# Up projection of an encoder layer: a third seven-product pair in every second group, and both transposed sets of a group in one place

## The chip, the cores and the metric

The kernel runs on one core of a Trainium2 chip. The metric is the device time of one execution in microseconds, taken as the median of several runs. The engines are TensorE (PE in the profile, with its weight loads shown as PEld), VectorE (DVE), ScalarE (ACT), GpSimd (POOL) and SyncE (SP), which here only issues DMAs.

## The reference

One layer of an encoder on 256 tokens of width 2048, all in float32. The part that matters here is the last one, the squared-ReLU MLP between two RMS norms; ahead of it come two attention branches with gates.

```
h = rms_norm(x, norm_mix_pre)
proj = h @ w_in                       # q, k, v of two attentions, two gates
oa, on = diff_attention(...), neighbourhood_attention(...)
mixed = sigmoid(g_a) * (oa @ w_branch_a) + sigmoid(g_b) * (on @ w_branch_b)
x = x + rms_norm(mixed @ w_out, norm_mix_post)
h = rms_norm(x, norm_mlp_pre)
u = square(relu(h @ w_up))            # w_up is 2048 x 8192
x = x + rms_norm(u @ w_down, norm_mlp_post)
```

## The kernel before, in words

**Products.** Each float32 operand is split into a high part that TensorE takes in its rounded format and a low part, the rest. A product of two operands is then three matmuls: high by high, high by low, low by high (`Products.add`, L695 to L706). A matmul here has 128 x 128 elements of the activations as its stationary operand and 128 x 512 of the weights as its moving one.

**Groups and pairs.** The up projection (L1100 to L1149) runs over eight groups of 1024 columns of `w_up`. In a group it runs over eight *pairs*: a pair is 256 of the 2048 rows, a weight tile of 128 x 4 x 512 (1 MB), and both token halves. A pair is taken in one of two ways. As a light pair (`eight`, L720) it has eight products, so 24 matmuls, into four PSUM banks. As a heavy pair (`seven`, L708) it is a 2 x 2 block product by the scheme of Strassen and Winograd: seven products, 21 matmuls, into seven banks, of which four (0, 4, 5, 6) belong to heavy pairs alone. For it VectorE has to form sums of the weight blocks (`pair_weights`, L644 to L660), and sums of the activations have to be there (`sums_of`, L768, kept in `h2sum`).

**The weights of a pair.** `pair_weights` (L633) loads the raw tile by a DMA on SyncE's queue. For a light pair ScalarE makes the high part (L640) and VectorE the low part (L642). For a heavy pair three quarters of the tile are split so (L645, L649), and four sums of 512 columns are made by VectorE (L646 to L648, tile `t`) and split as well (L658 by ScalarE into `eh`, L659 by VectorE into `el`). There are three buffers each for the raw, the high and the low tile. The split sums lie in the pool `mid` of five buffers, four to a heavy pair, unless a `low` is given: then the two low sums lie there. `Weights.next` (L672) asks for the weights of two pairs ahead of the one to be computed.

**The end of a group.** After the last heavy pair of a group `combine` (L726) puts the heavy banks together into the tile `z` with one copy by ScalarE and four adds by VectorE (L729 to L733). After the last light pair `u_piece` (L1094) adds each of the four light banks to `z` on VectorE (L1097) and applies ReLU and the row's scale on ScalarE (L1098). The next group's light products need these four banks.

**Transposes.** The down projection needs the squared result with its columns on the partitions. While group g runs, `u_sets` (L1076) does this for the two 512-column halves of group g - 1: eight TensorE transposes into two PSUM banks for each half (L1084), a square by ScalarE (L1087), then the splits and, for the even half, the sums of the down projection's heavy pairs (`act_sets`, L1019), and DMAs on GpSimd's queue that keep the results in device memory (L1046). The banks of the transposes come from the pool of four that also holds the heavy pairs' own banks.

**Pages.** Most working tiles, `z`, the transposed sets, the weight sums `t` and the `h2sum` among them, come from one pool of 27 buffers of 4 KB a partition (`page`).

**Order.** The list `UPS` (L1100) gives the pairs of a group in order, each with 1 if it is heavy; group 0 takes all its pairs light (`ALL8`). In `wide_group` (L735) a place n of that list first calls for weights, then `each(n)` (here `up_each`, L1123, which calls `u_sets` in the second and third place), then the products. Each engine's queue is ordered when the program is built, by the kernel's order and a simulated timeline; at run time each queue goes in its order, and waits by semaphores. So matmuls of neighbouring pairs can stand mixed in TensorE's queue.

Of the kernel before, what the change touches and what calls it, by code (L numbers as in the profile page):

```python
# [50 lines left out]
def encoder_layer(ctx: ExitStack, tc: tile.TileContext, a, out):  # L51
# [13 lines left out]
    def page(shape, dt, name):  # L65
        return pages.tile(shape, dt, tag="pg", name=name)
# [7 lines left out]
    def bank(name, big=False):  # L74
        if big:
            return mm.tile([P, 512], F32, tag="mm", name=name)
        return ms.tile([P, 512], F32, tag="ms", name=name)
# [602 lines left out]
    def columns(src, i, c):  # L680
        return src[i * T : (i + 1) * T, c : c + 1024].rearrange("(k p) c -> p k c", p=P)
# [53 lines left out]
    def wide_group(name, kinds, weights, stat7, stat8, mm_banks, z, piece, each=None, turn=None, after={}, in_order=False):  # L735

        any7 = any(s for _, s in kinds)
        pr = Products(name, mm_banks)  # L740
        pr.in_order = in_order
        for n, (i, seven) in enumerate(kinds):
            w = weights.next(after)
            if each:
                each(n)
            if seven:
                final = not any(s for _, s in kinds[n + 1 :])
                pr.seven(partial(stat7, i), w, final)
                if final:
                    pr.combine(z)  # L750
                continue
            end = n == len(kinds) - 1
            if turn and n < 2:
                ahead = [*ahead, (i, w)] if n else [(i, w)]
                for t in range(2) if n else ():
                    for ii, ww in ahead:
                        for which in (2 * t, 2 * t + 1):
                            pr.eight(partial(stat8, ii), ww, which, False)
                    if not t:
                        turn()  # L760
                continue
            for which in range(4):
                pr.eight(partial(stat8, i), w, which, end)
                if end:
                    b, t, half = PLAIN[which]
                    piece(t, half, pr.ps[b], any7)

    def sums_of(p1, p2, name):  # L768

        a11, a21, a12, a22 = p1[:, :P], p1[:, P:], p2[:, :P], p2[:, P:]  # L770
        s = page([P, 4, P], F32, f"{name}s")
        nc.vector.tensor_sub(s[:, 0], a21, a22)
        nc.vector.tensor_sub(s[:, 1], a11, a21)
        nc.vector.tensor_sub(s[:, 2], s[:, 0], a11)
        nc.vector.tensor_add(s[:, 3], a12, s[:, 2])
        parts_ = page([P, 2, 4, P], F32R, name)
        nc.scalar.copy(parts_[:, 0], s)
        nc.vector.tensor_sub(parts_[:, 1], s, parts_[:, 0].bitcast(F32))
        return parts_
# [24 lines left out]
    ALL8 = [(i, 0) for i in range(8)]  # L804
# [193 lines left out]
    def first_up(n):  # L998
        for t, c in {2: [(1, 1), (0, 2)], 3: [(1, 2), (0, 3)], 4: [(1, 3)]}.get(n, ()):
            residual_parts(t, c)  # L1000
        if n == 5:
            for t in range(2):
                mlp_squares(t)
                mlp_scale(t)
            for i in range(4):
                kd = dram.tile([P, 1024], F32, name=f"keepx{i}", tag=f"keepx{i}")
                nc.gpsimd.dma_start(kd, x2[i])
                kept["x", i] = kd
# [10 lines left out]
    def act_sets(cg, u):  # L1019


        srcs = []
        if seven_of(cg):
            a11, a21 = u[:, 0:2, :P], u[:, 0:2, P:]
            a12, a22 = u[:, 2:4, :P], u[:, 2:4, P:]
            sums = page([P, 4, 2, P], F32, f"sm{cg}")
            nc.vector.tensor_sub(sums[:, 0], a21, a22)
            nc.vector.tensor_sub(sums[:, 1], a11, a21)
            nc.vector.tensor_sub(sums[:, 2], sums[:, 0], a11)
            nc.vector.tensor_add(sums[:, 3], a12, sums[:, 2])  # L1030
            own = [(slice(0, 1), a11.unsqueeze(1)),
                   (slice(1, 3), u[:, 2:4].rearrange("p k (t q) -> p t k q", t=2))]
            if cg in FIRST:
                own.append((slice(3, 4), a21.unsqueeze(1)))
            srcs = [([P, 1 + len(own), 2, P], own), ([P, 4, 2, P], [(slice(0, 4), sums)])]
        else:
            srcs = [([P, 4, T], [(slice(0, 4), u)])]
        got = []
        for i, (shape, pieces) in enumerate(srcs):
            hi, lo = page(shape, F32R, f"ah{cg}{i}"), page(shape, F32R, f"al{cg}{i}")  # L1040
            for at, src in pieces:
                nc.scalar.copy(hi[:, at], src)
                nc.vector.tensor_sub(lo[:, at], src, hi[:, at].bitcast(F32))
            for n, part in (("h", hi), ("l", lo)):
                kd = dram.tile(shape, F32, name=f"keep{n}{cg}{i}", tag=f"keep{n}{cg}{i}")
                nc.gpsimd.dma_start(kd, part.bitcast(F32))  # L1046
                kept[cg, i, n] = (shape, kd)
            got.append([hi, lo])
        return got
# [26 lines left out]
    def u_sets(cg, z):  # L1076

        u = page([P, 4, T], F32, f"u{cg}")
        for b in range(2):
            pt = bank(f"uT{cg}{b}")  # L1080
            for j in range(2):
                for t in range(2):
                    c = (b * 2 + j) * P
                    nc.tensor.transpose(  # L1084
                        pt[:, j * T + t * P : j * T + (t + 1) * P], z[t][:, cg % 2, c : c + P], ident
                    )
            nc.scalar.activation(  # L1087
                u[:, b * 2 : b * 2 + 2], pt.rearrange("p (j q) -> p j q", j=2), AF.Square
            )
        got = act_sets(cg, u)  # L1090
        if NG - 4 <= cg < NG - 2:
            sets[0, cg] = got
# [4 lines left out]
            nc.vector.tensor_add(zt, zt, ps)  # L1097
        nc.scalar.activation(zt, zt if summed else ps, AF.Relu, scale=r2[:, t : t + 1])  # L1098

    UPS = [(0, 0), (1, 0), (2, 0), (3, 1), (4, 0), (5, 1), (6, 0), (7, 0)]  # L1100
    uw = Weights()
    for g in range(DFF // 1024):
        for i, seven in UPS if g else ALL8:
            uw.ask(columns(a["w_up"], i, g * 1024), f"u{g}_{i}", seven)
    wd = a["w_down"].rearrange("(g h j p) c -> p h g j c", h=2, j=2, p=P)

    blocks = [[NG - 4] + list(range(0, NG - 4, 2)) + [NG - 2], [NG - 2] + list(range(0, NG - 2, 2))]
# [11 lines left out]
    uz = None  # L1119
    for g in range(DFF // 1024):  # L1120
        z = Late(lambda g=g: [page([P, 2, 512], F32, f"u{g}{t}") for t in range(2)])

        def up_each(n, g=g, uz=uz):  # L1123
            if not g:
                first_up(n)
                if n == 7:
                    for i in (3, 5):
                        f = page([P, 2, T], F32, f"h2f{i}")
                        for k in range(2):
                            d = hT2[i][:, k].bitcast(F32)  # L1130
                            nc.vector.tensor_add(f[:, k], d[:, :T], d[:, T:])
                        h2sum[i] = sums_of(f[:, 0], f[:, 1], f"h2s{i}")
            elif n in (1, 2):
                u_sets(g * 2 - 3 + n, uz)

        wide_group(
            f"u{g}",
            UPS if g else ALL8,
            uw,
            h2stat7,  # L1140
            h2stat8,
            (1, 2, 3, 7),
            z,
            partial(u_piece, z=z),
            each=up_each,
            turn=None if g else turn_rows,
            after={} if g else {1: tail[1][1], 2: scaled[0]},
        )
        uz = z  # L1149
# [149 lines left out]
```

## Time and profile before

| | |
|---|---|
| runs | 1358.05, 1360.42, 1361.4 us; median 1360.42 us |
| profiled execution | 1359.99 us, span of its trace 1358.2 us |
| granted TensorE clock | 0.996, mean over the span |
| matmul instructions | 6336 |
| device memory traffic | 335.85 MB, mean 247 GB/s |
| VectorE, ScalarE busy | 1031.9 us, 716.9 us |

The span runs from the first to the last instruction; the profiled execution's own time has 1.8 us around it. In rows of groups the columns are: line, engine, operation, output<-inputs, shapes, count, then busy time and mean of one in ns, then idle time of the engine ahead of them with what ended it. In rows of a timeline they are: start, duration, engine, line and so on, with idle time in brackets. In rows of the chain of waits: start, duration, engine, tile, line, count. L12 is line 12 of the kernel.

### The profile page before, as it was taken

Reading aid. Unit: us, or ns where it says so; the run is one execution under the profiler, and the core shown is the slowest. Engines: PE = TensorE matmul, PEld = TensorE weight load, DVE = VectorE, ACT = ScalarE, POOL = GpSimd, SP = SyncE. Lnnn points to the kernel's source line nnn. Section 1 sums busy time; section 2 is a strip of 40 time slices with the busy share of each in tenths; the row PEclk is TensorE's granted clock in tenths of the full one; section 3 lists DMA queues with packets and bytes.
Section 4 is the critical chain, followed back from the end, with each engine's and each line's share of the span. In section 5 each row is a group of like instructions: output and inputs, shape, how many; then the busy total and the mean of one; then the engine's idle time right before and its main releaser. Section 6 shows DMA issues by size and latency. Waiting matters only on the chain.

```text
span 1358.2 us, 16184 instructions
## 1 busy us (share of the span) xinstructions
PE 1339.8 (99%) x6336; PEld 1120.5 (82%) x6336; DVE 1031.9 (76%) x1176; ACT 716.9 (53%) x841; POOL 38.1 (3%) x71
## 2 busy tenths in 40 slices
PE   8999999999999999999999999999999999999996
PEld 7888888888888888888788888878888888888885
DVE  6878866767867886655777887787888988788886
ACT  6655454545644454344575655556565545555452
POOL 0000000000000000000100000000000000000000
PEclk9999999999999999999999999999999999999999
DMA  9774745574556655575668767776699998799894
GB/s 316 256 235 163 206 159 174 168 205 154 191 186 199 216 204 186 185 281 187 212 204 287 239 227 261 271 248 232 248 322 335 372 358 336 273 361 371 313 370 179
DMA packets 116588, 335.85 MB, mean 247 GB/s; under 512 B 16928, under 2 KB 17440, under 8 KB 116512
## 3 DMA queue, kind: packets, MB, share of 16 engines
q1 hardware_dynamic: 95888, 264.03, 56.8%
q10 hardware_dynamic: 13904, 45.10, 8.7%
q0 software_dynamic: 6720, 25.69, 4.7%
q8 instruction: 49, 0.80, 0.2%
q14 instruction: 27, 0.22, 0.0%
HBM read 307.01 MB, written 29.61 MB: 248 GB/s over the span
## 4 chain that ended last, share of the span: by engine, by line
PE 90%; DMA 5%; DVE 2%; ACT 2%; issue 1%; SPq 0%; ACTq 0%; DVEq 0%; POOLq 0%
PE p L702 24%; PE u L702 21%; PE ga L702 6%; PE gb L702 6%; PE ba L702 3%; PE bb L702 3%; PE qn_p L212 2%; PE kn_p L212 2%; PE y_p L255 2%; PE y_p L254 2%; PE y_p L256 2%; DMA u_0r<-in_w_up 2%; PE qn_p L214 1%; PE kn_p L214 1%; PE ka_p L212 1%; PE qa_p L212 1%
## 5 line engine op out<-in xcount | busy, mean ns | idle before, releaser
L138 DVE TENSOR_TENSOR y_l<-y_w,y_h 128x1024 fp32r<-128x1024 f32 x32 | 37.9, 1222 | 30.9 <-ACT y_h L133 30.9
L133 ACT CAST y_h<-y_w 128x1024 fp32r<-128x1024 f32 x32 | 32.1, 1051 | 40.9 <-PE y_p L256 32.5
L212 PE MATMUL ka_p<-hT,ka_h 128*128 128x512 f32 x128 | 46.9, 410 | 3.3 <-DVE rope_s L281 3.3
L254 PE MATMUL y_p<-y_h,mh 128*128 128x512 f32 x128 | 50.1, 391 | 0.0
L255 PE MATMUL y_p<-y_l,mh 128*128 128x512 f32 x128 | 49.9, 390 | 0.0
L256 PE MATMUL y_p<-y_h,ml 128*128 128x512 f32 x128 | 49.8, 390 | 0.0
L702 PE MATMUL u<-u_0h,h2T 128*128 128x512 f32 x128 | 44.5, 392 | 1.7 <-DVE u L1097 1.6
L212 PE MATMUL qn_p<-hT,qn_h 128*128 128x512 f32 x128 | 45.9, 400 | 0.0
L212 PE MATMUL kn_p<-hT,kn_h 128*128 128x512 f32 x128 | 45.4, 398 | 0.0
L212 PE MATMUL qa_p<-hT,qa_h 128*128 128x512 f32 x128 | 44.9, 407 | 0.4 <-DVE hT L293 0.3
L702 PE MATMUL u<-u_1h,h2T 128*128 128x512 f32 x128 | 44.0, 397 | 0.0
L702 PE MATMUL u<-u_6h,h2T 128*128 128x512 f32 x128 | 41.8, 389 | 0.0
L702 PE MATMUL u<-u_2h,h2T 128*128 128x512 f32 x128 | 41.7, 396 | 0.0
L702 PE MATMUL u<-u_7h,h2T 128*128 128x512 f32 x128 | 41.7, 389 | 0.0
L702 PE MATMUL u<-u_4h,h2T 128*128 128x512 f32 x128 | 41.2, 391 | 0.0
L214 PE MATMUL ka_p<-hT,ka_l 128*128 128x256 f32 x128 | 36.1, 287 | 0.0
L214 PE MATMUL qn_p<-hT,qn_l 128*128 128x256 f32 x128 | 35.9, 281 | 0.0
L214 PE MATMUL kn_p<-hT,kn_l 128*128 128x256 f32 x128 | 35.7, 280 | 0.0
L640 ACT CAST u_1h<-u_1r 128x2048 fp32r<-128x2048 f32 x8 | 15.3, 1916 | 35.6 <-PE u L702 31.6
L214 PE MATMUL qa_p<-hT,qa_l 128*128 128x256 f32 x128 | 33.3, 281 | 0.3 <-DVE qa_l L138 0.3
L212 PEld LDWEIGHTS ka_p<-hT,ka_h 128*128 128x128 f32 x128 | 24.7, 194 | 9.3 <-DVE rope_s L281 3.6
L642 DVE TENSOR_TENSOR u_0l<-u_0r,u_0h 128x2048 fp32r<-128x2048 f32 x8 | 18.3, 2292 | 17.0 <-ACT u_0h L640 17.0
(1379 smaller groups left out, 4364.3 us busy)
## 6 DMA issues: line engine op xcount, KB each, us to landing
y_w<-in_w_out SPq DMA_DIRECT2D x16, 1024.0 KB, 5.2
bh<-keeph ACTq DMA_DIRECT2D x30, 512.0 KB, 9.4
bl<-keepl ACTq DMA_DIRECT2D x30, 512.0 KB, 11.1
keeph<-ah POOLq DMA_DIRECT2D x18, 512.0 KB, 8.0
keepl<-al POOLq DMA_DIRECT2D x18, 512.0 KB, 9.0
ka_w<-in_w_in SPq DMA_DIRECT2D x8, 1024.0 KB, 6.4
va_w<-in_w_in SPq DMA_DIRECT2D x8, 1024.0 KB, 5.2
qn_w<-in_w_in SPq DMA_DIRECT2D x8, 1024.0 KB, 5.2
```

The costliest lines, as they stand in the source:

```text
L133: nc.scalar.copy(hi[part], raw[part])
L138: sub = nc.vector.tensor_sub(lo[part], raw[part], hi[part].bitcast(F32)).ins
L212: nc.tensor.matmul(ps[b], hi[:, k % 4, cs], mv, start=(k == 0), stop=False)
L214: nc.tensor.matmul(ps[b][:, :T], lo[:, k % 4, cs], mv[:, :T], start=False, stop=(k == nk - 1))
L254: nc.tensor.matmul(ps[t], sh, hi[:, k % 4], start=(k == 0), stop=False)
L255: nc.tensor.matmul(ps[t], sh, lo[:, k % 4], start=False, stop=False)
L256: nc.tensor.matmul(ps[t], sl, hi[:, k % 4], start=False, stop=(k == nk - 1))
L640: nc.scalar.copy(h1, raw)
L642: nc.vector.tensor_sub(l1, raw, h1.bitcast(F32))
L702: ins = nc.tensor.matmul(self.ps[i], st, mv[:, blk], start=i not in self.begun, stop=last and n == 2).ins
```

## The change

In groups 2, 4 and 6 the list of pairs becomes another one, with three heavy pairs (0, 3 and 5) in the third, fifth and seventh place. Groups 1, 3, 5 and 7 keep their list with two heavy pairs in the fourth and sixth place, and group 0 keeps its eight light pairs. The activation sums of pair 0 are made in group 0 beside those of 3 and 5. Both transposed sets of the group before are called for in the second place of a group; before, the second set was called for in the third. And the low parts of the weight sums of all the up projection's heavy pairs are put in pages (`page` as `low`) and no longer in `mid`.

```diff
-    UPS = [(0, 0), (1, 0), (2, 0), (3, 1), (4, 0), (5, 1), (6, 0), (7, 0)]
+    UPS = [
+        [(0, 0), (1, 0), (2, 0), (3, 1), (4, 0), (5, 1), (6, 0), (7, 0)],
+        [(1, 0), (2, 0), (0, 1), (4, 0), (3, 1), (6, 0), (5, 1), (7, 0)],
+    ]
+
+    def ups(g):
+        return UPS[g % 2 == 0] if g else ALL8
+
     uw = Weights()
     for g in range(DFF // 1024):
-        for i, seven in UPS if g else ALL8:
-            uw.ask(columns(a["w_up"], i, g * 1024), f"u{g}_{i}", seven)
+        for i, seven in ups(g):
+            uw.ask(columns(a["w_up"], i, g * 1024), f"u{g}_{i}", seven, page)
...
                 if n == 7:
-                    for i in (3, 5):
+                    for i in (0, 3, 5):
                         f = page([P, 2, T], F32, f"h2f{i}")
...
-            elif n in (1, 2):
-                u_sets(g * 2 - 3 + n, uz)
+            elif n == 1:
+                for i in range(2):
+                    u_sets(g * 2 - 2 + i, uz)
 
         wide_group(
             f"u{g}",
-            UPS if g else ALL8,
+            ups(g),
             uw,
```

## The prediction

> **What bounds the kernel now.** I read the page's totals first, then who TensorE waits for, then the chain of waits.
>
> ```profile
> PE 1339.8 (99%) x6336; PEld 1120.5 (82%) x6336; DVE 1031.9 (76%) x1176; ACT 716.9 (53%) x841; POOL 38.1 (3%) x71
> ```
> ```profile
> PE u L702 <- DVE u L1097: 1.6, 1, 1.6
> ```
> ```profile
> 354.62 41.48 PE gb L702 x183
> ...
> 439.62 41.48 PE ga L702 x183
> ...
> 717.97 38.59 PE u L702 x170
> ...
> 805.38 0.66 PE uT L1084 x6
> ```
>
> TensorE (PE) is the bound: it is busy 99% of the span, and in the eight groups of the up projection the only sizeable wait that ends at it is one of 1.6 us. A busy row alone could hide slow issue, so I take the pace from the chain: 183 products in 41.48 us and 170 in 38.59 us are both 0.227 us a product. This pace does not vary, so what shortens the kernel is fewer products, provided that the operands come in time. What could spoil that is read in the up stage, group by group (columns: PE, PEld, DVE, ACT, POOL busy, clock, DMA share, GB/s):
>
> ```profile
> 661.80:704.90 43.10, 43.10 (x202) 35.68 (x203) 31.93 (x54) 27.77 (x52) 4.80 (x5) 1.00 0.64 218
> ...
> 749.10:793.50 44.40, 44.40 (x205) 36.80 (x205) 34.46 (x35) 24.93 (x25) 3.22 (x6) 1.00 0.73 255
> ...
> 837.50:883.00 45.50, 45.49 (x209) 37.39 (x207) 35.53 (x35) 27.37 (x26) 3.22 (x6) 1.00 0.71 248
> 883.00:928.00 45.00, 43.37 (x199) 35.97 (x200) 37.24 (x36) 25.04 (x26) 3.21 (x6) 1.00 0.72 251
> 928.00:972.00 44.00, 44.00 (x204) 36.41 (x203) 35.85 (x35) 25.84 (x26) 3.21 (x6) 1.00 0.73 257
> ```
> ```profile
> 439.60:481.10 41.50, 41.50 (x185) 34.37 (x184) 36.13 (x34) 22.12 (x17) 0.00 (x0) 1.00 0.60 203
> ```
>
> The second window is group 2, the third about group 4, the fifth about group 6: the groups that get the third heavy pair. VectorE (DVE) is the next engine, with some 34.5 to 35.9 us of work in 44. The last line is a gate group that has three heavy pairs in eight already, without transposes: DVE 36.13 of 41.50 us (87%), PE without a gap.
>
> **The change part by part.** *Products.* A light pair is 24 products, a heavy one 21. Groups 2, 4 and 6 each turn one light pair into a heavy one: 3 x 3 = 9 products less, 9 x 0.227 = 2.04 us less of PE. No product of another group changes. The Trainium skill ("TensorE: Matmul & The Clock Gate", Part 1, under "Wait — 56ns, not 53.3ns?") gives 215.7 ns for a warm product of 512 columns; by it the term would be 1.94 us. The chain's 0.227 us is the measured pace here and decides.
>
> *Weight work.* The rows of group 2 by shape:
>
> ```profile
> L642 DVE TENSOR_TENSOR u_1l<-u_1r,u_1h 128x2048 fp32r<-128x2048 f32 x1 | 2.3, 2286 | 0.0
> ...
> L658 ACT CAST u_5eh<-u_5t 128x1024 fp32r<-128x1024 f32 x2 | 2.1, 1050 | 3.7 <-DVE u_5t L646 3.7
> ...
> L640 ACT CAST u_1h<-u_1r 128x2048 fp32r<-128x2048 f32 x1 | 1.9, 1918 | 6.9 <-PE u L702 6.9
> ...
> L649 DVE TENSOR_TENSOR u_5l<-u_5r,u_5h 128x1536 fp32r<-128x1536 f32 x1 | 1.8, 1761 | 0.2 <-ACT u_5h L645 0.2
> ...
> L645 ACT CAST u_5h<-u_5r 128x1536 fp32r<-128x1536 f32 x1 | 1.5, 1477 | 0.0
> ...
> L646 DVE TENSOR_TENSOR u_5t<-u_5r 128x1024 f32<-128x1024 f32 x1 | 1.2, 1219 | 0.0
> ...
> L648 DVE TENSOR_TENSOR u_5t<-u_5t,u_5r 128x512 f32<-128x512 f32 x1 | 0.7, 693 | 0.0
> ```
>
> On DVE a light pair costs 2.29 us. A heavy one costs 1.22 (L646) + 2 x 0.69 (L647, L648) + 1.76 (L649) + two L659 of 128x1024, the shape of L646, 2 x 1.22: 6.80 us. So each of the three groups gets 4.51 us more on DVE. ScalarE (ACT) goes from 1.92 to 1.48 + 2 x 1.05 = 3.58 us, 1.66 more: about 26.6 of 43.7 us in group 2, no limit. DVE in those groups comes to 39 to 40.4 us of 43.3 (44.0 less 3 x 0.227): 90 to 93%, above the 87% that the gate group shows to be harmless. Averaged over an even and an odd group it is (2 x 35.9 + 4.5) of 87.3 us, 87% again, and since loads are asked for two pairs ahead some backlog can move into the odd group. So by throughput DVE fits, with about 3 us to spare in an even group. I take zero for it; its bounds are below.
>
> *The sums for pair 0.* One more set in group 0: two adds of 128x256, four of 128x128, one split of 128x512.
>
> ```profile
> 688.63 0.75 DVE L1131 TENSOR_TENSOR h2f<-h2T 128x256 f32<-128x256 f32 x2
> 689.56 0.28 DVE L773 TENSOR_TENSOR h2s3s<-h2f 128x128 f32<-128x128 f32 x1
> ...
> 697.31 0.68 DVE L778 TENSOR_TENSOR h2s<-h2s3s,h2s 128x512 fp32r<-128x512 f32 x1
> ```
>
> 0.75 + 4 x 0.28 + 0.68 = 2.6 us of DVE, where the group has 43.10 - 31.93 = 11.2 us free: nothing. Uncovered it could cost its 2.6 us once.
>
> *Transposes together.* Their count stays. Six take 0.66 us, and all sixteen 1.8 us, as before. They now need four PSUM banks at once, all four of the pool that the heavy products' extra sums use, one pair ahead of the heavy pair in third place. That heavy pair waits for four squares on ACT. There is a full light pair (24 x 0.227 = 5.44 us) between, so I count nothing; without that cover it is the wait for those squares, under 3 us in each of three groups. The keep writes that GpSimd issues behind the second set start earlier and move against the weight loads on SyncE's queue, whose own issues wait for raw buffers that the splits free:
>
> ```profile
> 862.22 11.11 DMA u_0r<-in_w_up
> ```
> ```profile
> u_4r<-in_w_up SPq DMA_DIRECT2D x5, 1024.0 KB, 5.0
> ```
> ```profile
> 875.30 2.29 DVE L642 TENSOR_TENSOR u_0l<-u_0r,u_0h 128x2048 fp32r<-128x2048 f32 x1 [4.12 <-ACT u_0h L640]
> 877.51 0.68 DVE L730 TENSOR_TENSOR u<-u,u 128x512 f32<-128x512 f32 x1
> 878.23 0.69 DVE L731 TENSOR_TENSOR u<-u,u 128x512 f32<-128x512 f32 x1
> 878.83 0.68 DVE L1097 TENSOR_TENSOR u<-u,u 128x512 f32<-128x512 f32 x1
> ...
> 882.75 1.23 DVE L646 TENSOR_TENSOR u_3t<-u_3r 128x1024 f32<-128x1024 f32 x1 [2.04 <-DMA u_3r<-in_w_up]
> 883.89 1.28 DVE L1097 TENSOR_TENSOR u<-u,u 128x512 f32<-128x512 f32 x2
> ```
>
> This is the 1.6 us gap of TensorE: u_0r took 11.11 us where an undisturbed load takes 5.0; u_3r could start only when u_0l had freed its buffer; DVE stood 2.04 us at the add on u_3r, and behind it in the queue stood two of the pieces (L1097) that free the banks for group 5. Whether the shifted writes hit that load again I cannot read, so the gap stays in my sum; it may go (-1.6) or double (+1.6).
>
> *The low sums in pages.* They leave the pool of five buffers, of which one heavy pair took four, for the shared pages: two pages more for each heavy pair. No time of its own.
>
> *The last heavy pair in seventh place.* The combine (L729 to L733) had the sixth place with two light pairs behind it; in even groups it now has one, 5.44 us.
>
> ```profile
> 789.07 0.69 DVE L730 TENSOR_TENSOR u<-u,u 128x512 f32<-128x512 f32 x1 [2.69 <-PE u L702]
> ```
> ```profile
> 793.18 0.39 PE L702 MATMUL u<-u_0h,h2T 128*128 128x512 f32 x1
> ```
> ```profile
> 862.11 1.22 DVE L1043 TENSOR_TENSOR al<-u,ah 128x1024 fp32r<-128x1024 f32 x1
> 863.24 1.22 DVE L646 TENSOR_TENSOR u_5t<-u_5r 128x1024 f32<-128x1024 f32 x1
> ```
> ```profile
> 469.69 0.68 DVE L730 TENSOR_TENSOR ga<-ga,ga 128x512 f32<-128x512 f32 x1
> ```
>
> Group 3 begins at 793.18; two light pairs back, 782.3, is where group 2's last heavy pair would end in strict order. Its combine began at 789.07, 6.8 us late, and cost nothing, as the products of the last pairs were mixed in. In the gate group, which ends at 439.62 + 41.48 = 481.10, the same point is 470.2 and the combine came at 469.69, not late. I read the difference so: in the up stage the second heavy pair's first add follows the split of the second transposed set directly (862.11, 863.24), as if its pages were given out only behind that set's. With the sets together at an earlier place and the seventh place two heavy pairs away from them, I expect the combine late by 0 to 3 us, nearer the gate's row. If it is late by s, group end is 5.44 - s later, and the first bank is free after an add, a piece and an activation, 0.7 us each: the wait is s - 3.3 us, so none.
>
> *Sum.* 1359.99 (the profiled execution: span 1358.2 and 1.8 around it) - 2.04 = 1357.95, say 1358.0. That execution lies 0.43 us under the median of the runs, 1360.42.
>
> **The rivals.** *Gap closed too.* The early keep writes miss u_0r, and the 1.6 us go: 1359.99 - 2.04 - 1.6 = 1356.3. For it: two of three even-to-odd boundaries show no such gap. Against: the same bytes move.
>
> *Combine too late (slower).* If the seventh-place pair slips by the 6.8 us of group 2's sixth, PE waits 6.8 - 3.3 = 3.5 us at the end of groups 2, 4 and 6, one of which holds the old 1.6: 1359.99 - 2.04 + 10.5 - 1.6 = 1366.9. It decides from a slip over 3.3 us, and costs more than the gain from one of 4.5 on (3 x 1.2 against 2.04 + 1.6). For it: DVE at 90 to 93%, with combine (2.75), pieces (2.75), one light split (2.29) and an add (1.2) in the last 5.44 us. Against: the gate group. A rule of the Trainium skill would make it worse ("TensorE: Matmul & The Clock Gate", "HAM oscillation"): idle gaps above about 3.4 us halve the matmul clock for the next window, by my estimate up to 1.7 us more for each gap. The one gap here, 1.6 us, left the clock at 1.00; no run shows a longer one in this stage.
>
> *Loads late, spread out.* A heavy pair holds its raw buffer longer, and each even group loses a gap like the present 1.6: 1359.99 - 2.04 + 2 x 1.6 = 1361.2.
>
> **How the numbers follow.** 0.3% of 1360 is 4.1 us, about what a measurement can tell from no change. Chances: forecast 0.53, gap closed 0.14, loads late 0.14, combine too late 0.19. Forecast and late loads are within 0.3%; so is the closed gap, but with the runs' scatter (1358.05 to 1361.4) it gives most of 0.10 for faster. Slower: 0.19 and a little of the late loads, 0.20. Same: 0.70. The range starts at the closed gap less 0.8 of scatter, 1355.5, and reaches half way into the late combine, 1364.5.
>
> **What would show it.** In the profile after: 9 products of L702 fewer; three heavy pairs by L646 in groups 2, 4, 6; DVE near 40 us there; PE's waits in the up stage at most about 2 us; L730 in even groups no more than 3 us after the pair's place. A wait of PE for L1097 at the ends of groups 2, 4 and 6 would show the forecast wrong, and a wait of the third-place heavy pair for L1087 would show the bank cover wrong.

## The result and the profile after

The changed kernel takes 1373.37 us (median of 4 runs, 1370.0 to 1377.11), the kernel before in the same comparison 1359.24 us. The ratio is 1.0103, 95% interval 1.0088 to 1.0117: slower by 1.0%, where a gain of 2 us was forecast. The trace below has a span of 1373.4 us, 15.2 us longer than before.

The totals of the page after, and TensorE's waits (who waited for whom: us in total, times, longest):

```profile
PE 1341.6 (98%) x6327; PEld 1119.2 (81%) x6327; DVE 1044.6 (76%) x1198; ACT 723.4 (53%) x848; POOL 38.1 (3%) x71
```
```profile
PE u L702 <- DVE u_2l L642: 7.7, 5, 2.9
PE u L702 <- DVE u L1097: 4.9, 3, 1.7
...
PE p L702 <- DMA bl<-keepl: 1.9, 2, 1.7
...
PE u L702 <- DVE u_5el L659: 0.9, 1, 0.9
```

The nine products are gone: 6327 matmuls for 6336. But where the up stage had one wait of 1.6 us, it now has 7.7 + 4.9 + 0.9 = 13.5 us of them. Nearly all of it stands at the ends of groups. These are the ends of groups 2, 3 and 4 in TensorE's timeline, with the idle time in brackets:

```profile
793.64 0.50 PE L702 MATMUL u<-u_0h,h2T 128*128 128x512 f32 x1 [1.67 <-DVE u L1097]
798.17 0.50 PE L702 MATMUL u<-u_2l,h2T 128*128 128x512 f32 x1 [1.27 <-DVE u_2l L642]
842.30 0.50 PE L702 MATMUL u<-u_2l,h2T 128*128 128x512 f32 x1 [1.12 <-DVE u_2l L642]
887.09 0.50 PE L702 MATMUL u<-u_0h,h2T 128*128 128x512 f32 x1 [1.53 <-DVE u L1097]
893.24 0.61 PE L702 MATMUL u<-u_2l,h2T 128*128 128x512 f32 x1 [2.90 <-DVE u_2l L642]
```

The end of group 2 loses 1.67 + 1.27 us, that of group 4 1.53 + 2.90. The end of the odd group 3 loses 1.12 with no wait for a piece. The gap of 2.90 us has a price of its own, seen in the granted clock (last column but two) of the two stretches behind it:

```profile
893.20:897.00 3.80, 3.76 (x10) 2.95 (x11) 3.80 (x6) 1.57 (x3) 0.00 (x0) 0.55 0.71 226
897.00:900.40 3.40, 3.40 (x17) 2.78 (x16) 1.54 (x2) 1.43 (x2) 0.00 (x0) 1.00 0.16 60
```

For 3.8 us after it the clock is 0.55; the chain of waits has 23 products in 7.11 us there, 1.9 us more than at 0.227.

Most of the sum can be followed with the first products of two stages, before and after (first and last start):

```profile
L702 PE MATMUL u<-u_0h,h2T x128: 387/389/501, 657.6 to 981.2; 128*128 128x512 f32 x128
...
L702 PE MATMUL p<-d0130h,ah x8: 389/389/476, 1015.7 to 1020.9; 128*128 128x512 f32 x8
...
L702 PE MATMUL p<-d1150h,bh x8: 389/389/389, 1182.8 to 1187.6; 128*128 128x512 f32 x8
```
```profile
L702 PE MATMUL u<-u_0h,h2T x92: 387/390/629, 656.9 to 995.8; 128*128 128x512 f32 x92
...
L702 PE MATMUL p<-d0130h,ah x8: 389/389/389, 1028.5 to 1033.2; 128*128 128x512 f32 x8
...
L702 PE MATMUL p<-d1150h,bh x8: 389/389/389, 1198.1 to 1202.8; 128*128 128x512 f32 x8
```

From the up projection's first product to the down projection's first it took 358.1 us before and 371.6 after: 13.5 more. Of that are 11.9 the new waits (13.5 less the old 1.6), 1.9 the slow clock, -2.0 the products; 1.7 are left over, some of it the slower first products after each gap (0.34 us in place of 0.23). From there to the first product of d1150h, with which the down projection's second half begins, it is 167.1 against 169.6 us: 1.9 of these 2.5 us are waits for a kept set to come back from device memory. TensorE was 0.7 us ahead when the up projection began.

Now VectorE's queue through group 2, and the last product that the combine's first add (L730) needs:

```profile
759.93 2.29 DVE L642 TENSOR_TENSOR u_4l<-u_4r,u_4h 128x2048 fp32r<-128x2048 f32 x1 [4.83 <-ACT u_4h L640]
...
770.28 1.22 DVE L1043 TENSOR_TENSOR al<-u,ah 128x1024 fp32r<-128x1024 f32 x1
771.41 1.22 DVE L646 TENSOR_TENSOR u_3t<-u_3r 128x1024 f32<-128x1024 f32 x1
...
779.88 1.22 DVE L659 TENSOR_TENSOR u_3el<-u_3t,u_3eh 128x1024 fp32r<-128x1024 f32 x1
781.01 1.22 DVE L646 TENSOR_TENSOR u_5t<-u_5r 128x1024 f32<-128x1024 f32 x1
...
788.13 1.22 DVE L659 TENSOR_TENSOR u_5el<-u_5t,u_5eh 128x1024 fp32r<-128x1024 f32 x1
789.38 2.29 DVE L642 TENSOR_TENSOR u_1l<-u_1r,u_1h 128x2048 fp32r<-128x2048 f32 x1
791.59 0.68 DVE L730 TENSOR_TENSOR u<-u,u 128x512 f32<-128x512 f32 x1
792.30 0.69 DVE L731 TENSOR_TENSOR u<-u,u 128x512 f32<-128x512 f32 x1
792.91 0.68 DVE L1097 TENSOR_TENSOR u<-u,u 128x512 f32<-128x512 f32 x1
...
795.84 2.28 DVE L642 TENSOR_TENSOR u_2l<-u_2r,u_2h 128x2048 fp32r<-128x2048 f32 x1
...
798.64 0.68 DVE L1097 TENSOR_TENSOR u<-u,u 128x512 f32<-128x512 f32 x1
```
```profile
789.74 0.39 PE L702 MATMUL u<-u_5eh,h2s 128*128 128x512 f32 x1
```

Read it backward. The low sums of the third heavy pair (u_5el) are done at 789.35. TensorE's products of the group end at 793.64 - 1.67 = 791.97, so the seventh place ends in strict order a light pair earlier, at 786.53: the sums come after the place is over. They come late because u_5t follows the end of pair 3's sums, and u_3t follows directly behind the split of the second transposed set. VectorE stood idle for 4.83 us at 755, as the head of its queue waited for u_4h from ScalarE. From 749.10 to 793.50 it was busy 36.5 of 44.4 us, less than the 39 that the prediction summed.

The combine follows at 791.59, 5.1 us late, and the sums are not all of the reason. The products of the last heavy pair stand among those of the last light pair in TensorE's queue. The one shown ends at 790.13, 3.6 us behind the strict end of the place. The combine's first add then waits 1.5 us more, because a split of the next group (u_1l) stands directly ahead of it in VectorE's queue. Behind the first piece stands another split of the next group (u_2l), ahead of the other pieces. At the ends of groups 4 and 6 u_1l stands in the same place.

### The profile page after: what moved, and what is told of

It is laid out like the page before. It is cut to its first block, busy times and chain, and to the rows that moved or that the text cites. A ratio compares the mean times of both kernels' runs of the same rounds, so it can differ in the third digit from the quotient of the medians.

```text
span 1373.4 us, 16192 instructions
## 1 busy us (share of the span) xinstructions
PE 1341.6 (98%) x6327; PEld 1119.2 (81%) x6327; DVE 1044.6 (76%) x1198; ACT 723.4 (53%) x848; POOL 38.1 (3%) x71
## 4 chain that ended last, share of the span: by engine, by line
PE 89%; DVE 5%; DMA 3%; ACT 1%; issue 1%; ACTq 0%; SPq 0%; DVEq 0%; POOLq 0%
PE p L702 21%; PE u L702 20%; PE ga L702 6%; PE gb L702 6%; PE ba L702 3%; PE bb L702 3%; PE ka_p L212 2%; PE qn_p L212 2%; PE kn_p L212 2%; PE y_p L256 2%; PE y_p L254 2%; PE y_p L255 2%; PE qa_p L212 2%; DMA bl<-keepl 1%; PE ka_p L214 1%; PE qn_p L214 1%
## 5 line engine op out<-in xcount | busy, mean ns | idle before, releaser
L702 PE MATMUL u<-u_0h,h2T 128*128 128x512 f32 x92 | 33.6, 406 | 4.9 <-DVE u L1097 4.9
L702 PE MATMUL u<-u_2l,h2T 128*128 128x512 f32 x64 | 25.9, 404 | 7.7 <-DVE u_2l L642 7.7
L1098 ACT ACTIVATE u<-u,r 128x512 f32<-128x512 f32 x32 | 22.0, 715 | 19.5 <-DVE u L1097 18.0
```

The costliest lines, as they stand in the source:

```text
L702: ins = nc.tensor.matmul(self.ps[i], st, mv[:, blk], start=i not in self.begun, stop=last and n == 2).ins
```

## The experiments

All ratios are to the kernel before, run on the same chip in the same set of runs. Two theories stood at first. A: the third heavy pair gives VectorE more than it can do in time. B: the side edits, the joined transposed sets and the low sums in pages, push the weight sums back.

**Without the third pair.** The kernel before with both side edits:

```diff
-            uw.ask(columns(a["w_up"], i, g * 1024), f"u{g}_{i}", seven)
+            uw.ask(columns(a["w_up"], i, g * 1024), f"u{g}_{i}", seven, page)
...
-            elif n in (1, 2):
-                u_sets(g * 2 - 3 + n, uz)
+            elif n == 1:
+                for i in range(2):
+                    u_sets(g * 2 - 2 + i, uz)
```

> The two side edits alone: both transposed sets in the second place and the low weight sums in pages, but the old list of two heavy pairs in every group. Theory A (VectorE has too much to do in a group with three heavy pairs): within 2 us of before, and TensorE's waits in the up stage stay near 1.6 us. Theory B (the side edits push the weight sums behind the transposed set's pages): 5 us or more slower than before.

1358.09 us, ratio 0.9987 (0.9973 to 1.0001). The side edits cost nothing by themselves; B falls as the cause. The waits were not as A expected: the profiled execution (1361.99 us, 3.9 above the median) has two waits for a split (u_1l) at the ends of groups 3 and 5, 3.4 us together, and not the old one of 1.6.

**The third pair alone.** The changed kernel with the side edits undone: sets in the second and third place, low sums in the pool of five.

```diff
-            uw.ask(columns(a["w_up"], i, g * 1024), f"u{g}_{i}", seven, page)
+            uw.ask(columns(a["w_up"], i, g * 1024), f"u{g}_{i}", seven)
...
-            elif n == 1:
-                for i in range(2):
-                    u_sets(g * 2 - 2 + i, uz)
+            elif n in (1, 2):
+                u_sets(g * 2 - 3 + n, uz)
```

> The third heavy pair alone, in third, fifth and seventh place; the transposed sets stay in the second and third place and the low sums in the pool of five. Theory A: as slow as the changed kernel, about 1370 to 1376 us. Theory B: near before, 1357 to 1362 us. If the pool of five buffers, of which three heavy pairs take twelve, is the narrower place, slower than the changed kernel.

1371.72 us, ratio 1.0074 (1.0051 to 1.0096), with the same kinds of wait:

```profile
PE u L702 <- DVE u L1097: 6.6, 3, 2.3
PE u L702 <- DVE u_2l L642: 3.0, 3, 1.3
```

The third pair carries most of the loss without the side edits.

**The changed kernel with one side edit undone.** First the low sums (the first line of the diff above), then the transposed sets (the rest of it).

> The changed kernel with the low weight sums back in the pool of five. Theory A: 1370 to 1376 us, as the work on VectorE is the same. Theory B (pages): at least 4 us faster than the changed kernel.

1370.91 us, ratio 1.0068 (1.0048 to 1.0088): a third of the loss goes, by ratios whose intervals just touch. The time lies in A's range, but by the ratios some 4.8 us less are lost, which is what B asked for; this run alone does not separate the two.

> The changed kernel with the transposed sets in the second and third place again. Theory A: 1370 to 1378 us; the second set's work on VectorE comes later and so nearer to the third pair's sums, a little slower rather than faster. Theory B (the joined sets): at least 4 us faster than the changed kernel.

1377.62 us, ratio 1.0119 (1.0095 to 1.0142). The joined sets do no harm. With them apart TensorE waits for the third pair's sums themselves (u_5el 5.0 us, u_5eh 2.3). This kernel and the third pair alone differ by the low sums only, and again the one with pages is the slower (1.0119 against 1.0074). So the low sums in pages, free with two heavy pairs, add to the loss with three, but neither side edit is its root.

So what about the third pair costs the time: VectorE's work as such, the pages behind the transposed set, the order of the queue at the end, or the seventh place? Four kernels changed one of these each.

**The same work, the last heavy pair in sixth place.**

```diff
-        [(1, 0), (2, 0), (0, 1), (4, 0), (3, 1), (6, 0), (5, 1), (7, 0)],
+        [(1, 0), (2, 0), (0, 1), (3, 1), (4, 0), (5, 1), (6, 0), (7, 0)],
```

> The changed kernel with the heavy pairs of even groups in the third, fourth and sixth place: the combine has two light pairs behind it again, the work on VectorE is the same. Theory P (the seventh place leaves the combine too little time): within 3 us of before, no wait of TensorE for L1097 at the ends of even groups. Theory A (VectorE has too much to do in an even group): 1367 us or more; the waits stay or move.

1357.89 us, ratio 0.9985 (0.9973 to 0.9997): 2 us faster than before with all of the third pair's work in place, as the change was forecast to be. All of TensorE's waits in groups 1 to 7:

```profile
PE u L702 <- DVE u_2l L642: 0.5, 1, 0.5
PE u L702 <- DVE u L1097: 0.3, 1, 0.3
```

The list moves two pairs, and both moves show. In VectorE's queue the first add of the second heavy pair now stands ahead of the transposed set, as its place comes before; the third pair's sums are done at 784.1, and the combine still comes late:

```profile
754.76 1.22 DVE L646 TENSOR_TENSOR u_3t<-u_3r 128x1024 f32<-128x1024 f32 x1
...
782.86 1.22 DVE L659 TENSOR_TENSOR u_5el<-u_5t,u_5eh 128x1024 fp32r<-128x1024 f32 x1
...
789.58 0.69 DVE L730 TENSOR_TENSOR u<-u,u 128x512 f32<-128x512 f32 x1
...
796.40 2.29 DVE L642 TENSOR_TENSOR u_1l<-u_1r,u_1h 128x2048 fp32r<-128x2048 f32 x1
```

Group 3 begins at 794.14 in this kernel. Two light pairs back is 783.26, so the combine is 6.3 us late, later than the changed kernel's 5.1; but two light pairs cover it. The split of u_1l now comes behind the combine. VectorE's load alone is not the cause.

**Less work, the seventh place kept.** TensorE reads the high sums where it read the low ones in groups 2, 4 and 6.

```diff
-                    part.append(low(shape, F32R, n))
+                    part.append(h2[i] if name[:3] in ("u2_", "u4_", "u6_") else low(shape, F32R, n))
...
-            nc.vector.tensor_sub(l2[i], t[i], h2[i].bitcast(F32))
+            if name[:3] not in ("u2_", "u4_", "u6_"):
+                nc.vector.tensor_sub(l2[i], t[i], h2[i].bitcast(F32))
```

> The low parts of the weight sums are not made in groups 2, 4 and 6; TensorE takes the high parts in their place, so its products are as many and the output is not the reference's there. VectorE has 6 x 1.22 = 7.3 us less to do in each of the three groups, less than before the change. Theory A (VectorE's load): 1356 to 1359 us, the gain that was forecast. Theory P (the seventh place): at least 5 us above before, as the combine still comes behind the seventh place.

1361.57 us, ratio 1.0016 (1.0006 to 1.0027): between the two, in neither theory's range. Most of the loss goes with 7.3 us less to do in each even group, yet 2 us above before stay, and 4 us above the forecast. The edit also leaves six pages free in each even group, so it does not tell work from pages.

**Own buffers for the sums t.**

```diff
-    pages = ctx.enter_context(tc.tile_pool(name="pages", bufs=27))
+    pages = ctx.enter_context(tc.tile_pool(name="pages", bufs=24))
...
-        t = [page([P, 2, 512], F32, f"{name}t{i}") for i in range(2)]
+        t = [mid.tile([P, 2, 512], F32, tag="t", name=f"{name}t{i}", bufs=3) if name[0] == "u" else page([P, 2, 512], F32, f"{name}t{i}") for i in range(2)]
```

> In the up projection the weight sums t get three buffers of their own, and the pages are three fewer (24); so the second and third pair's first adds need not wait for the pages of the transposed set. Same work. If VectorE is late because its adds are queued behind the transposed set: TensorE's waits in the up stage fall from 13.5 us to under 7 us. If it is late by its load alone: 11 us or more of waits stay. The 24 pages may cost some us in other stages, so the up stage is read by itself.

1359.79 us, ratio 1.0006 (0.9997 to 1.0016). Pair 3's first add goes into the idle time that the changed kernel had at 755, and of TensorE's waits in groups 1 to 7 one kind is left:

```profile
757.85 1.22 DVE L646 TENSOR_TENSOR u_3t<-u_3r 128x1024 f32<-128x1024 f32 x1 [0.93 <-DMA u_3r<-in_w_up]
...
792.55 2.29 DVE L642 TENSOR_TENSOR u_1l<-u_1r,u_1h 128x2048 fp32r<-128x2048 f32 x1 [1.15 <-ACT u_1h L640]
794.76 0.68 DVE L730 TENSOR_TENSOR u<-u,u 128x512 f32<-128x512 f32 x1
```
```profile
PE u L702 <- DVE u L1097: 5.0, 3, 1.9
```
```profile
796.91 0.47 PE L702 MATMUL u<-u_0h,h2T 128*128 128x512 f32 x1 [1.87 <-DVE u L1097]
```

So it was the shared pages that kept the sums behind the transposed set; that pages are handed out in the order of the program fits this. With that gone 8.5 of the 13.5 us go, and what goes are the waits for u_2l and u_5el: in VectorE's queue the pieces now stand ahead of u_2l. The first wait at each even end stays, 5.0 us for 4.9. The third pair's sums are done at 788.5 here, 1.1 us before the strict end of their place, and still the combine is 5.2 us late. It stands behind u_1l, which waits for ScalarE.

**The pieces ahead of the next split.** In odd groups the low part of the third pair is queued behind the last piece of the group before.

```diff
-            nc.vector.tensor_add(zt, zt, ps)
+            last_piece[0] = nc.vector.tensor_add(zt, zt, ps).ins
...
-            after={} if g else {1: tail[1][1], 2: scaled[0]},
+            after=({8 * g + 2: last_piece[0]} if last_piece[0] else {}) if g else {1: tail[1][1], 2: scaled[0]},
```

> The changed kernel, but the low part of the third pair of a group (light, in odd groups) is queued on VectorE behind the last piece of the group before. Same work. If the order of the queue makes the loss (the split of 2.29 us between the pieces): the waits at the ends of even groups fall from about 3 to 4.5 us to under 2 us each, 1366 us or less. If VectorE is simply late there: the same waits under other names, 1371 us or more.

1365.95 us, ratio 1.0051 (1.0034 to 1.0067). The first wait stays at what it was, the second shrinks to 0.3 us at even ends; the last lines are the combine in VectorE's queue and the split ahead of it:

```profile
PE u L702 <- DVE u L1097: 5.7, 6, 1.7
...
PE u L702 <- DVE u_2l L642: 0.5, 1, 0.5
```
```profile
797.44 0.50 PE L702 MATMUL u<-u_0h,h2T 128*128 128x512 f32 x1 [1.72 <-DVE u L1097]
```
```profile
793.18 2.29 DVE L642 TENSOR_TENSOR u_1l<-u_1r,u_1h 128x2048 fp32r<-128x2048 f32 x1 [0.45 <-ACT u_1h L640]
795.39 0.68 DVE L730 TENSOR_TENSOR u<-u,u 128x512 f32<-128x512 f32 x1
```

So the place of u_2l in the queue makes about half of the loss, not all of it. The place of u_1l, ahead of the combine, was not changed here, and no run changed it alone.

**Two heavy pairs, one in the seventh place.** Is the place enough by itself?

```diff
-        [(1, 0), (2, 0), (0, 1), (4, 0), (3, 1), (6, 0), (5, 1), (7, 0)],
+        [(1, 0), (2, 0), (0, 0), (4, 0), (3, 1), (6, 0), (5, 1), (7, 0)],
```

> The changed kernel with pair 0 light again in its third place: even groups have two heavy pairs, in the fifth and the seventh place. VectorE has no more to do than before the change, TensorE the same 6336 matmuls. Theory P (the seventh place alone, whatever the load): waits of TensorE for L1097 and the following split at the ends of groups 2, 4 and 6 as in the changed kernel, 1365 us or more. If the place costs only together with late sums of a third pair: no such waits, 1357 to 1361 us.

1358.68 us, ratio 0.9987 (0.9976 to 0.9998). TensorE has no wait in groups 1 to 7. The combine of group 2 and the first product of group 3, which follows without idle time:

```profile
787.59 2.29 DVE L642 TENSOR_TENSOR u_1l<-u_1r,u_1h 128x2048 fp32r<-128x2048 f32 x1 [0.22 <-ACT u_1h L640]
789.80 0.68 DVE L730 TENSOR_TENSOR u<-u,u 128x512 f32<-128x512 f32 x1
```
```profile
791.95 0.46 PE L702 MATMUL u<-u_0h,h2T 128*128 128x512 f32 x1
```

The place alone costs nothing, but at the end of group 2 only just: the first piece ends at 791.80, 0.15 us before it is needed. Four kernels, all with both side edits, make a table of two by two. With two heavy pairs the ratio is 0.9987 when the last one has the sixth place and 0.9987 when it has the seventh; with three it is 0.9985 and 1.0103. In every second group, neither the third pair's work nor the seventh place is slow; only both together are.

**Three heavy pairs in every group.** The list with the sixth place, in groups 1 to 7.

```diff
-        return UPS[g % 2 == 0] if g else ALL8
+        return UPS[1] if g else ALL8
```

> Groups 1 to 7 all take three heavy pairs, in the third, fourth and sixth place: 4 x 3 = 12 products fewer than with even groups alone, 2.7 us. VectorE has about 40 us of work in every group of 43.3 and no lighter group to recover in. Theory P (only the seventh place hurt; load has slack): 1353 to 1356 us. Theory A (VectorE's load is the limit at about 93%): waits of TensorE return at 2 us a group or more, 1360 us or above.

1365.55 us, ratio 1.0043 (1.0029 to 1.0056). Four waits, nearly all of it three of 2.53 us at the ends of groups 2, 4 and 6, two of them followed by a low clock. Below are the waits, the window of group 3, and idle time of VectorE ahead of the end of group 2:

```profile
PE u L702 <- DVE u_2l L642: 8.0, 4, 2.5
```
```profile
793.00:837.00 44.00, 41.47 (x185) 34.16 (x184) 39.73 (x40) 27.11 (x27) 3.23 (x6) 0.96 0.73 257
```
```profile
784.19 2.29 DVE L642 TENSOR_TENSOR u_1l<-u_1r,u_1h 128x2048 fp32r<-128x2048 f32 x1 [4.18 <-ACT u_1h L640]
```

By the number this is theory A's outcome, with VectorE at 39.7 us in 44 (90%) in this window. That its load is the limit is not shown: it stood idle for 4.18 us before the end of group 2, waiting for ScalarE, and the split that TensorE waited for (u_2l) stands in its queue behind the combine, a piece and the next heavy pair's first adds. One heavy pair more in the odd groups does cost time; whether by load or by order stays open.

## Why the prediction was wrong

*The products.* Right in the trace: nine fewer, and with the sixth place the way from the first product of the up projection to the first of the down projection is 355.0 us, 3.1 less than before, of which 2.0 are the products and 0.8 shorter waits. The time alone does not show it: the two kernels with all 6336 products and two heavy pairs came to 0.9987, as good as the 0.9985.

*The weight work.* Right in kind: the load as such fits in every second group. VectorE's total rose by 12.7 us where 3 x 4.51 + 2.6 = 16.1 were summed. In the timeline instructions that follow each other overlap by some 0.08 us (789.38 + 2.29 is 791.67, and the next begins at 791.59), and there are 22 more of them; that is about half of the difference. Taking zero for it was wrong in one way: the load was weighed as an average over a group, while what counted was when the last sums were ready.

*The combine.* This step failed: "I expect the combine late by 0 to 3 us, nearer the gate's row." It was 5.1 us late. The reading under it was right, that the sums' pages come behind the transposed set's (own buffers moved u_3t from 771.41 to 757.85). The conclusion was not. A distance of two pairs did not bring the sums in time: u_5t follows pair 3's sums, and the last one was done 2.8 us behind the strict end of its place. Nor are late sums enough as the reason: with own buffers they were in time, and the combine was 5.2 us late. What the traces show in its place are two things that the prediction left out of its account. The heavy pair's products are mixed among those of the last light pair, so that the one the combine needs ends 3.6 us late by the same count; the prediction had seen this mixing in group 2 and taken it as harmless. And the split of u_1l stands ahead of the combine, which adds 1.5 us. In the kernel before, and with the sixth place, the add begins at the end of group 2 as soon as its product is there (0.04 us behind it in both). The row of group 2, 6.8 us, was nearer than the gate's.

*The threshold.* Right in size, in part by luck. With one light pair behind the combine the wait was to be s - 3.3 us; with two, 5.44 us less. The prediction counted an add, a piece and an activation, 0.7 us each. The rows show two adds and a piece (791.59, 792.30, 792.91, end 793.59), and TensorE goes on at 793.64 without an activation. The sum is the same.

| kernel, end of group 2 | combine | products end | late by s | s - 3.3 | first wait |
|---|---|---|---|---|---|
| changed | 791.59 | 791.97 | 5.1 | 1.8 | 1.67 |
| own buffers | 794.76 | 795.04 | 5.2 | 1.9 | 1.87 |
| pieces first | 795.39 | 795.72 | 5.1 | 1.8 | 1.72 |
| two pairs, seventh | 789.80 | 791.95 | 3.3 | 0.0 | none |
| sixth place | 789.58 | 794.14 | 6.3 | none, 8.7 to spend | none |
| low sums in the pool of five | 789.25 | 791.02 | 3.7 | 0.4 | 2.37 |

It holds in the first five rows and fails in the last. There u_1l stands between the first add and the second, and no longer ahead of the first, so the combine begins earlier, but its second add and the first piece do not come earlier:

```profile
789.25 0.69 DVE L730 TENSOR_TENSOR u<-u,u 128x512 f32<-128x512 f32 x1 [1.78 <-PE u L702]
789.86 2.29 DVE L642 TENSOR_TENSOR u_1l<-u_1r,u_1h 128x2048 fp32r<-128x2048 f32 x1
```

The third pair alone has the same order there, and a wait of 2.32 us.

*The rival "combine too late"* was the one that came, at 0.19. Its price was too low, 10.5 us for 13.5 and what followed. It stopped at the first wait; it did not see that in VectorE's queue a split for the next group stands between the pieces (the second wait, 1.27 to 2.90 us), nor the 1.12 us at each of the two odd ends ahead of a group with three heavy pairs, nor the waits in the down projection. So the time lay above the range's end of 1364.5, and above the rival's own 1366.9.

*The clock.* The rival's sentence on the Trainium skill set the point at about 3.4 us of idle time. Here the clock fell after less, below.

*The side edits.* The transposes and the pair-0 sums are right: no wait for L1087, no new one in group 0. The low sums in pages were taken at no time of their own; with three heavy pairs they make about a third of the loss (1.0103 against 1.0068, and 1.0119 against 1.0074). *The old gap* of 1.6 us at group 4's end: a wait for L1097 stands there still, of 1.53 us, and whether it has the old cause was not settled.

What stays open: 1.7 us of the up stage's 13.5 are not assigned; no run moved the split of u_1l behind the combine and nothing else; and why the kept sets came back later in the down projection was not tried.

## What to carry to other kernels

An engine with room on average can still be late at one point: price a step by when its last input is ready, by what stands ahead of it in its engine's queue, and by how much other work lies between it and whoever needs its result, here two light pairs that cover 8.7 us against one that covers 3.3. Where several edits come together, run each alone before blaming the load: here a third heavy pair was free in an earlier place and the seventh place was free with two, and moving the second and third heavy pair one place forward turned 1.0103 into 0.9985. And look at what hands out shared buffers: a tile of an urgent step that is allotted behind a leisurely one waits for it, even with VectorE idle.

## What the runs showed of the hardware

TensorE's clock fell after shorter gaps than expected, and not after each. In the kernel with the third pair alone a gap of 2.32 us and one of 2.13 us were followed by 3.5 us at 0.65 and 0.51, and a third, of 2.13 us, by none. With two pairs and the seventh place a gap of 1.50 us in the down projection, closely behind one of 0.50, was followed by 3.5 us at 0.52. These are the stretches after the two gaps of 2.13 us and after the one of 1.50:

```profile
887.90:891.40 3.50, 3.43 (x8) 2.75 (x9) 3.50 (x5) 1.77 (x2) 0.00 (x0) 0.51 0.65 259
980.90:984.40 3.50, 3.24 (x13) 2.36 (x13) 3.50 (x4) 1.78 (x2) 0.00 (x0) 1.00 0.66 261
```
```profile
1060.00:1063.50 3.50, 3.47 (x8) 2.80 (x9) 3.03 (x4) 0.18 (x2) 0.00 (x0) 0.52 0.88 352
```

After the gaps of 1.6 us before the change, of 1.67 and 1.53 us after it and of 1.87 us with own buffers the clock stayed at 1.00. The Trainium skill ("TensorE: Matmul & The Clock Gate", "HAM oscillation") names about 3.4 us as the gap to avoid. In these runs gaps of 1.50 to 2.90 us were followed by a low clock in some places and not in others, so the length of one gap does not decide it; what does is not shown.
